# A hybrid encoder layer on one core: where a product is added in the first two column pairs, and at what pace the second batch's attention is issued

## The chip, the core and the metric

One NeuronCore of one Trainium2 chip. The core has a matrix engine (TensorE, PE in the profile), three engines for element-wise work (VectorE or DVE, ScalarE or ACT, GpSimd or POOL), a queue that issues transfers (SyncE or SP), and sixteen DMA engines. The metric is device time of one execution in microseconds (us), as the median of three runs.

## What is computed

Two batches, a "prompt" of 512 rows and a "sample" of 1024 rows, both 1024 wide, go through one layer with shared weights, in float32:

```python
h = rmsnorm(x); z = h @ w_in                # columns: q, k, v, conv a, conv b
a_out = window_attention(q, k, v)           # |q-k| <= 128, 8 heads, 2 kv heads, bias table, sink
c = silu(layernorm(dwconv31(ca * sigmoid(cb))))
x = x + concat(a_out, c) @ w_out
h = rmsnorm(x)
u = dwconv3(h @ w_up)                       # 2 * 2816 columns: gates, then values
x = x + (silu(u_gate) * u_value) @ w_down
y = rmsnorm(x)
```

## The kernel before

**Products.** A float32 product is made of three matmuls on a split of each operand into a rounded part and a remainder: hi·hi, hi·lo, lo·hi. A split is a cast on ScalarE (the hi part) and a subtraction on VectorE or GpSimd (the lo part). A matmul has 128x128 weights and 512 moving columns.

**Stages.** (1) Input projections of both batches, with the prompt's attention and convolution between them. (2) The prompt's output projection. (3) The prompt's up-projection, 22 steps `ffn_step(k)`, each with a gate and a value column block of 128. The sample's attention and the rest of its long convolution are issued between these matmuls. (4) The sample's output projection: for each block `i` of 128 rows two halves of 512 columns (`out_half`, lines 796 to 798), after `conv_norm` of that block. (5) The sample's up-projection, 22 column pairs `j`, by a Winograd form of Strassen's method: seven products per pair (`first` to `seventh`, lines 1221 to 1223) in place of eight. (6) The down-projection of both batches, and the last norm.

**What sets the order.** In stages 1 to 4 the program is written with a pace: `tick()` is called between groups of matmuls, adds `pace["rate"]` to a credit, and for each whole unit of credit draws one step from the deque `side`. A scheduler then orders the instructions of each engine by its own model of their times, so that the written order is only a wish there. In stage 3 `side` holds `sample()`: 100 steps of the sample's attention (`scores`, `values`), then the loads and splits of `w_out` (`load_cat`, `split_wo`), then `conv_norm` of the first two sample blocks (`fitted(4)`, `fitted(5)`). `tick()` is called 8 times per step `k`, and the rate is RD = 0.55. The deque `late` holds the rest of the sample's convolution; it is empty from k = 19. Of the attention's 100 steps 83 are written by then, and 96 by the end of stage 3. Stage 4 then draws what is missing before its first block: 17 steps, the last of the attention, the loads and eight splits among them.

**The attention's chain.** Per pair of a block and a kv head: scores on TensorE (line 650); bias and row minimum on VectorE (654); exponential on ScalarE (663); reciprocal on VectorE (665); scaling on ScalarE (669) and GpSimd (671); transposes on TensorE (692); a split by ScalarE (694) and VectorE (695); values on TensorE (706, 707); copies out (714 to 718). Attention has three PSUM banks, a0 to a2. A split of `w_out` is a cast at line 828 and a subtraction at line 829.

**`conv_norm`.** Transposes on TensorE (755), statistics on VectorE (760, 761), a root on GpSimd (146, 147), scaling on VectorE (764), transposes back (770), four small scalings on ScalarE (776) and a tanh (777), then lines 778 (VectorE), 779 (ScalarE, hi part) and 780 (VectorE, lo part). Lines 755 and 770 write the banks a0 to a2 too. Of the eight weight blocks of an output half, the last four are the result of `conv_norm`; the first four come from the attention.

**The first two pairs.** At the start of stage 5 pairs 0 and 1 are written out side by side, and four engines keep the written order, between which the scheduler may still put later work. A pair has two double banks: `x` (gates) and `wy`, whose left half W takes the fifth and then the third product, and whose right half Y takes the sixth and seventh. `fifth(j)` ends with a ScalarE copy of W into SBUF, `p5` (1322). `y_sum(j)` adds `p5` to Y, `third(j)` accumulates onto W and adds `u2` to it; both additions are the VectorE line 1071, on the same tile `wy`. `gate_part(j)` reads `x` with one ScalarE pass (1337) and two VectorE passes (1338, 1339); when the last has read it, the bank of `x` is free, and `first(j + 2)` takes it. `sums_up(j)` are five subtractions at line 1074 on raw weights.

```python
def y_sum(j):
    Y = st[j]["wy"][:, R]
    add(Y, Y, st[j].pop("p5")[:])

def third(j):
    s = st[j]
    W = s["wy"][:, L]
    prod(W, j, 3, False, True)
    add(W, W, s.pop("u2")[:])
```

Of the kernel before, what the change touches and what calls it, by code (L numbers as in the profile page):

```python
# [39 lines left out]
RA, RB, RBO, RD, RN, RE = 1.2, 0.8, 2.5, 0.55, 0.8, 0.9  # L40
# [23 lines left out]
LK = 1  # L64
# [44 lines left out]
def tile_hybrid_encoder(ctx: ExitStack, tc: tile.TileContext, xs, rel_bias, norm_attn_g, w_in,  # L109
# [173 lines left out]
    mid = []  # L283
    side, pace = deque(), dict(rate=0.0, due=0.0, conv=0.0, credit=0.0, late=0.0)
# [44 lines left out]
    convs, late, kept = deque(), deque(), {}  # L329
# [673 lines left out]
    def ffn_step(k):  # L1003
        want_up_raw(k + 1, 1)
        ug = up_half(k, 0)
        want_up(k + 1, 0)
        uv = up_half(k, 1)
        want_up_raw(k + 2, 0)
        want_up(k + 1, 1)
        gate(k, ug[0], uv[0])  # L1010
# [15 lines left out]
    def sample():  # L1026
        for _ in units_of_sample:
            yield 0.0
            if at[0] >= KL and not wor:
                for kc in range(0, KC, 2):  # L1030
                    load_wo_pair(kc, 0)
        kt.clear(), vt.clear(), qt.clear(), bias.clear()
        use.update(norm="a")
        pace.update(rate=RN)
        load_cat(4)
        for kc in range(KC):
            load_wo(kc, 1)
            split_wo(kc, 0, kc % 4 < DW2)
            yield 0.0
        drain(late)  # L1040
        yield from fitted(4)
        for kc in range(KC):
            if kc == 2:
                load_cat(5)
            split_wo(kc, 1, kc % 4 < DW2)
            yield 0.0
            if kc == WN:
                yield from fitted(5)

    pace.update(rate=RD, late=0)  # L1050
    for k in range(NJ):
        at[0] = k
        if k == LK:
            pace.update(late=CD)
        if k == 0:
            side.append(sample())
        ffn_step(k)
# [12 lines left out]
    def add(out, a, b, eng=None):  # L1070
        (eng or nc.vector).tensor_tensor(out, a, b, op=ALU.add)  # L1071

    def sub(out, a, b, eng=None):
        (eng or nc.vector).tensor_tensor(out, a, b, op=ALU.subtract)  # L1074
# [105 lines left out]
    def block_up(j, half, k):  # L1180
        return uraw[j, half][:, 4 * k:4 * k + 4, :].rearrange("p k c -> p (k c)")
# [10 lines left out]
    def split_up(j, *which, apart=False):  # L1192
        if j >= NJ:
            return
        for i in which:
            if i == 7:
                held = third_sum.pop(j)
                src = held[:]
            else:
                src = block_up(j, *{1: (0, 0), 2: (0, 1), 6: (0, 0), 4: (0, 1), 5: (1, 0), 3: (1, 1)}[i])  # L1200
            if not apart and any(s[0][0] in "qc" for s in sb.free):
                t = sb.tile([2, NT], F32R)
                hi, lo = Part(t, 0), Part(t, 1)
            else:
                hi, lo = sb.tile([NT], F32R), sb.tile([NT], F32R)
            ops[j, i] = hi, lo
            nc.scalar.copy(hi[:], src)  # L1207
            sub(lo[:], src, hi[:].bitcast(F32), nc.gpsimd)
            held = None
            done.add((j, i))  # L1210
        for half, pair in ((0, (6, 4)), (1, (5, 3))):
            if (j, half) in uraw and all((j, i) in done for i in pair):
                uraw.pop((j, half))

    def prod(out, j, i, start, stop, between=None):
        whi, wlo = ops.pop((j, i))
        go = dict(skip_group_check=not start)
        for c in range(4):
            hi, lo = A[i, c]
            s = slice(c * P, (c + 1) * P)  # L1220
            nc.tensor.matmul(out, whi[:, s], hi[:], start=(start and c == 0), stop=False, **go)  # L1221
            nc.tensor.matmul(out, whi[:, s], lo[:], start=False, stop=False, **go)  # L1222
            nc.tensor.matmul(out, wlo[:, s], hi[:], start=False, stop=(stop and c == 3), **go)  # L1223
            if j == NJ - 1:
                A.pop((i, c))
            if between is not None:
                next(between, None)
# [89 lines left out]
    def fifth(j):  # L1317
        if j < NJ:
            s = st[j]
            prod(s["wy"][:, L], j, 5, True, True)  # L1320
            s["p5"] = sb.tile([NT])
            nc.scalar.copy(s["p5"][:], s["wy"][:, L])
# [11 lines that stand above are left out]
    def dwconv(src, f):  # L1334
        w = lambda t: fw[:, t * 44 + f:t * 44 + f + 1]
        u = sb.tile([W2])
        nc.scalar.activation(u[:], src[:], AF.Identity, scale=w(1), bias=fb[:, f:f + 1])
        nc.vector.scalar_tensor_tensor(u[:, 1:W2], src[:, 0:W2 - 1], w(0), u[:, 1:W2], op0=ALU.mult, op1=ALU.add)  # L1338
        nc.vector.scalar_tensor_tensor(u[:, 0:W2 - 1], src[:, 1:W2], w(2), u[:, 0:W2 - 1], op0=ALU.mult, op1=ALU.add)  # L1339
        return u  # L1340

    def gate_part(j):
        s = st[j]
        ug = s["ug"] = dwconv(s.pop("x"), j)
        t = s["t"] = sb.tile([W2])
        nc.scalar.activation(t[:], ug[:], AF.Tanh, scale=0.5)
# [113 lines left out]
    seventh(1, None, False)  # L1460
    sums_up(2)
    fifth(0)
    y_sum(0)
    gate_part(0)
    fifth(1)
    y_sum(1)
    by_hand.__exit__(None, None, None)
    by_hand = tc.manual_schedule(engines={mybir.EngineType.PE})
    by_hand.__enter__()
    gate_part(1)  # L1470
    third(0)
    split_up(2, 5)
    value_part(0)
    first(2)
    split_up(2, 6, apart=True)
    third(1)
    split_up(2, 7)
    fifth(2)
    split_up(2, 4, 3)
# [399 lines left out]
```

## Time and profile before

| what | value |
|---|---|
| runs | 1488.01, 1488.84, 1489.47 us; median 1488.84 |
| profiled execution | 1487.68 us, of which the span from first to last instruction is 1485.9 us |
| TensorE busy | 1467.1 us, 99% of the span, 6688 matmuls |
| VectorE busy | 1115.6 us, 75% |
| ScalarE busy | 807.7 us, 54% |
| GpSimd busy | 793.9 us, 53% |
| moved by DMA | 228.17 MB, 153 GB/s over the span |

Rows of instructions read: start in us from the span's start, duration in us, engine, line, operation, out<-in by the program's names (for a matmul: out<-moving,weights), shape, count. A bracket at the end is the time for which the engine was idle before it and what it waited for. Matmuls overlap in the array, so that a matmul's duration (0.39 us with 512 columns) is longer than the distance to the next one. A view of stretches has a row for each: its length, then each engine's busy time and number of instructions, then the TensorE clock that was granted (1.00 is full speed), the share of the DMA engines and GB/s.

### The profile page before, as it was taken

The page shows a single profiled execution, that of the slowest core. Times are in us where ns is not written, and L with a number is a line of the kernel's source. Part 1 is how long each engine was busy: PE and PEld are TensorE (multiplying, and loading weights), DVE is VectorE, ACT ScalarE, POOL GpSimd, SP SyncE. Part 2 cuts the span into 40 slices and gives each one's busy share as a digit, 9 for nine tenths or more (in the row PEclk, how much of TensorE's full clock was granted, in tenths as well). Part 3 has the DMA queues.
Part 4 walks back from the last instruction along what each step waited for, and adds up shares of the span by engine and source line. Part 5 has one row for each costly group of instructions (what it writes and reads, how often), then busy time and mean ns, then how long its engine had stood idle before and what let it go on. Part 6 is the DMA issues. An engine that isn't in the chain of part 4 may idle for free. (4 is left out here: it accounts for less than half of the span.)

```text
span 1485.9 us, 19792 instructions
## 1 busy us (share of the span) xinstructions
PE 1467.1 (99%) x6688; PEld 1207.9 (81%) x6688; DVE 1115.6 (75%) x1500; ACT 807.7 (54%) x1432; POOL 793.9 (53%) x697
## 2 busy tenths in 40 slices
PE   9999999999999999999999999999999999999998
PEld 7788887878888888778877888888888888888886
DVE  6877845648988888675598888888887856578873
ACT  7534555467778776654565455454455553433355
POOL 3564453338779766322547666666654341135556
PEclk9999999999999999999999999999999999999999
DMA  9555331844444454663114433333332394356744
GB/s 368 193 152 143 106 106 30 245 159 140 122 143 135 130 181 140 205 219 111 71 57 144 141 130 127 127 124 123 129 127 92 147 335 157 123 190 220 226 159 162
DMA packets 124624, 228.17 MB, mean 154 GB/s; under 512 B 20419, under 2 KB 45763, under 8 KB 124396
## 3 DMA queue, kind: packets, MB, share of 16 engines
q1 hardware_dynamic: 124092, 226.37, 46.6%
q8 instruction: 52, 0.85, 0.2%
q10 hardware_dynamic: 432, 0.56, 0.1%
q14 instruction: 48, 0.39, 0.1%
HBM read 166.83 MB, written 61.10 MB: 153 GB/s over the span
## 5 line engine op out<-in xcount | busy, mean ns | idle before, releaser
L163 POOL TENSOR_TENSOR q<-q,q 128x1024 fp32r<-128x1024 f32 x66 | 158.9, 2408 | 67.9 <-ACT q L162 42.9
L1074 POOL TENSOR_TENSOR q<-q,q 128x512 fp32r<-128x512 f32 x82 | 124.5, 1526 | 125.6 <-ACT q L1207 116.2
L1074 DVE TENSOR_TENSOR h<-h,h 128x512 fp32r<-128x512 f32 (+1 forms) x161 | 135.3, 870 | 55.9 <-ACT h L1082 23.4
L1575 PE MATMUL w<-h,h 128*128 128x512 f32 x432 | 168.1, 389 | 0.0
L1577 PE MATMUL w<-h,h 128*128 128x512 f32 x432 | 168.1, 389 | 0.0
L1576 PE MATMUL w<-h,h 128*128 128x512 f32 x412 | 160.3, 389 | 0.0
L1074 POOL TENSOR_TENSOR h<-h,h 128x512 fp32r<-128x512 f32 (+1 forms) x46 | 67.5, 1468 | 144.9 <-ACT h L1558 121.8
L1221 PE MATMUL w<-h,q 128*128 128x512 f32 x350 | 138.1, 394 | 3.7 <-DVE w L1071 3.2
L1223 PE MATMUL w<-h,q 128*128 128x512 f32 x350 | 136.4, 390 | 0.0
L1222 PE MATMUL w<-h,q 128*128 128x512 f32 x350 | 136.3, 389 | 0.0
L1082 ACT CAST h<-h 128x512 fp32r<-128x512 f32 x116 | 69.3, 620 | 103.5 <-DVE h L1074 35.2
L315 PE MATMUL b<-h,q 128*128 128x512 f32 x312 | 123.0, 395 | 1.2 <-ACT h L461 0.6
L317 PE MATMUL b<-h,q 128*128 128x512 f32 x312 | 122.6, 393 | 0.0
L316 PE MATMUL b<-h,q 128*128 128x512 f32 x312 | 122.3, 392 | 0.0
L315 PE MATMUL u<-h,q 128*128 128x512 f32 x272 | 106.8, 393 | 0.0
L316 PE MATMUL u<-h,q 128*128 128x512 f32 x272 | 106.8, 393 | 0.0
L317 PE MATMUL u<-h,q 128*128 128x512 f32 x272 | 106.7, 392 | 0.0
L162 ACT CAST q<-q 128x1024 fp32r<-128x1024 f32 x66 | 69.1, 1048 | 53.1 <-PE u L316 16.7
L352 DVE SCALAR_TENSOR_TENSOR c<-d,cvw,c 128x512 f32<-128x512 f32 x128 | 95.9, 749 | 1.6
L344 POOL TENSOR_TENSOR h<-h,h 128x512 f32<-128x512 f32 x62 | 81.6, 1318 | 27.1 <-ACT h L343 22.6
L1575 PEld LDWEIGHTS w<-h,h 128*128 128x128 f32 x432 | 81.1, 188 | 17.0
L1577 PEld LDWEIGHTS w<-h,h 128*128 128x128 f32 x432 | 81.1, 188 | 16.6
(462 smaller groups left out, 3995.5 us busy)
## 6 DMA issues: line engine op xcount, KB each, us to landing
q<-in_laid_w_up SPq DMA_DIRECT2D x88, 512.0 KB, 3.7
ga<-q SPq DMA_DIRECT2D x65, 256.0 KB, 2.3
h<-gap SPq DMA_DIRECT2D x57, 256.0 KB, 3.7
h<-ga SPq DMA_DIRECT2D x57, 256.0 KB, 3.6
h<-in_w_down SPq DMA_DIRECT2D x52, 256.0 KB, 3.5
q<-in_laid_w_in SPq DMA_DIRECT2D x22, 512.0 KB, 3.9
gap<-h SPq DMA_DIRECT2D x44, 256.0 KB, 2.3
q<-in_x_sample SPq DMA_DIRECT2D x15, 512.0 KB, 6.8
```

The source lines that it names most:

```text
L163: (nc.vector if dve else nc.gpsimd).tensor_tensor(lo[:], raw[:], hi[:].bitcast(F32), op=ALU.subtract)
L315: nc.tensor.matmul(out, whi[:, kc, :], hi[:], start=(kc == 0), stop=False)
L316: nc.tensor.matmul(out, whi[:, kc, :], lo[:], start=False, stop=False)
L317: nc.tensor.matmul(out, wlo[:, kc, :], hi[:], start=False, stop=(kc == KC - 1))
L352: nc.vector.scalar_tensor_tensor(acc[:], src(t), w(t), acc[:], op0=ALU.mult, op1=ALU.add)
L1074: (eng or nc.vector).tensor_tensor(out, a, b, op=ALU.subtract)
L1221: nc.tensor.matmul(out, whi[:, s], hi[:], start=(start and c == 0), stop=False, **go)
L1222: nc.tensor.matmul(out, whi[:, s], lo[:], start=False, stop=False, **go)
L1223: nc.tensor.matmul(out, wlo[:, s], hi[:], start=False, stop=(stop and c == 3), **go)
L1575: nc.tensor.matmul(out, sh[:, c], th[:], start=(p == 0 and not seeded), stop=False, **go)
L1576: nc.tensor.matmul(out, sh[:, c], tl[:], start=False, stop=False, **go)
L1577: nc.tensor.matmul(out, sl[:, c], th[:], start=False, stop=(p == NPAIR - 1), **go)
```

## The change

Two edits. The first sets the pace of `side` to RE = 0.9 in stage 3, as soon as `late` is empty and no convolution is open. That holds from k = 19, so that 90 steps of the attention are written before k = 20 (88 before the change), 98 before k = 21 (92), and at the end of stage 3 all 100 and the first four splits of `w_out`; stage 4 draws 9 steps before its first block in place of 17. The second edit writes `y_sum(j)` behind `third(j)` for j = 0 and 1, and `third(0)` ahead of `gate_part(1)`. Lines after 1055 have numbers that are higher by 2 in the changed kernel.

```diff
--- before.py
+++ after.py
@@ -1052,6 +1052,8 @@
         at[0] = k
         if k == LK:
             pace.update(late=CD)
+        if k > LK and not late and not mid:
+            pace.update(rate=RE)
         if k == 0:
             side.append(sample())
         ffn_step(k)
@@ -1460,20 +1462,20 @@
     seventh(1, None, False)
     sums_up(2)
     fifth(0)
-    y_sum(0)
     gate_part(0)
     fifth(1)
-    y_sum(1)
     by_hand.__exit__(None, None, None)
     by_hand = tc.manual_schedule(engines={mybir.EngineType.PE})
     by_hand.__enter__()
+    third(0)
+    y_sum(0)
     gate_part(1)
-    third(0)
     split_up(2, 5)
     value_part(0)
     first(2)
     split_up(2, 6, apart=True)
     third(1)
+    y_sum(1)
     split_up(2, 7)
     fifth(2)
     split_up(2, 4, 3)
```

What the scheduler makes of it is seen in three places. In the names below the first number is the buffer's, the last a running number.

**VectorE, first two pairs.** `w0` and `w1` are the banks `x` of pairs 0 and 1, `w2` and `w3` their `wy`; `q2`, `q12` are raw weights of pair 2, `q6`, `q7` and `h50_1338`, `q3` of pairs 3 and 4. Before:

```order
L1074 TENSOR_TENSOR q2_6_7791<-q2_6_7791,q12_5_7789 128x512
L1074 TENSOR_TENSOR q12_5_7789<-q2_6_7791 128x512
L1074 TENSOR_TENSOR q12_5_7789<-q12_5_7789 128x512
L1071 TENSOR_TENSOR w2_3_7739<-w2_3_7739,h50_1307_7899 128x512
L1338 SCALAR_TENSOR_TENSOR q14_1308_7902<-w0_1_7559,fw_264,q14_1308_7902 128x1023
L1074 TENSOR_TENSOR h50_1338_8184<-q3_10_8012 128x512
L1338 SCALAR_TENSOR_TENSOR q13_1311_7926<-w1_2_7574,fw_264,q13_1311_7926 128x1023
L1339 SCALAR_TENSOR_TENSOR q14_1308_7902<-w0_1_7559,fw_264,q14_1308_7902 128x1023
L1074 TENSOR_TENSOR q3_10_8012<-q3_10_8012,q10_9_8010 128x512
L1071 TENSOR_TENSOR w2_3_7739<-w2_3_7739,d0_1291_7793 128x512
L1339 SCALAR_TENSOR_TENSOR q13_1311_7926<-w1_2_7574,fw_264,q13_1311_7926 128x1023
```

And now:

```order
L1076 TENSOR_TENSOR q2_6_7791<-q2_6_7791,q12_5_7789 128x512
L1076 TENSOR_TENSOR q6_7_7857<-q7_8_7859 128x512
L1076 TENSOR_TENSOR q12_5_7789<-q2_6_7791 128x512
L1076 TENSOR_TENSOR q12_5_7789<-q12_5_7789 128x512
L1340 SCALAR_TENSOR_TENSOR q10_1308_7901<-w0_1_7559,fw_264,q10_1308_7901 128x1023
L1340 SCALAR_TENSOR_TENSOR q8_1311_7938<-w1_2_7574,fw_264,q8_1311_7938 128x1023
L1341 SCALAR_TENSOR_TENSOR q10_1308_7901<-w0_1_7559,fw_264,q10_1308_7901 128x1023
L1073 TENSOR_TENSOR w2_3_7739<-w2_3_7739,d0_1291_7793 128x512
L1341 SCALAR_TENSOR_TENSOR q8_1311_7938<-w1_2_7574,fw_264,q8_1311_7938 128x1023
L1073 TENSOR_TENSOR w2_3_7739<-w2_3_7739,h5_1307_7899 128x512
```

The addition of `p5` (`h50_1307`, now `h5_1307`) to `w2` stood ahead of the passes over `w0`; it now stands behind the addition of `u2` (`d0`). One subtraction for pair 3 (`q6<-q7`) has moved ahead of the two on `q12`, two for pair 4 have moved back, and the passes over `w0` and `w1` follow each other. TensorE keeps its order: fifth(0), fifth(1), third(0), first(2), third(1), fifth(2), each of 12 matmuls; the first matmul of third(0) and that of third(1) waited for VectorE and now wait for ScalarE.

**ScalarE, end of stage 3.** `u0_339` (now `u0_342`) is the last gate or value block of the prompt. Line 694 splits the transposed probabilities of the last but one attention unit. Before:

```order
L981 ACTIVATE b0_340_6421<-h40_1039_6377 128x512
L828 CAST h24_1075_6507<-q6_934_5671 128x512
L663 ACTIVATE h58_1026_6281,s5_1024_6271<-h58_1026_6281,s2_1023_6270 128x257
L828 CAST h32_1072_6501<-q6_934_5671 128x512
L828 CAST h16_1069_6495<-q12_933_5669 128x512
L828 CAST h12_1066_6489<-q12_933_5669 128x512
L965 ACTIVATE h33_1042_6416<-u0_339_6381,vecs_83,fw_264 128x512
L663 ACTIVATE h53_1028_6305,s5_1024_6271<-h53_1028_6305,s2_1023_6270 128x257
L694 CAST h7_1035_6351<-a1_336_6346 128x512
L663 ACTIVATE h54_1027_6299,s5_1024_6271<-h54_1027_6299,s2_1023_6270 128x257
L828 CAST h36_1089_6557<-h2_1056_6469 128x512
L694 CAST h22_1037_6366<-a2_337_6361 128x512
```

And now:

```order
L663 ACTIVATE h5_1023_6242,s5_1021_6232<-h5_1023_6242,s2_1020_6231 128x257
L694 CAST h56_1028_6285<-a1_333_6280 128x512
L663 ACTIVATE h54_1025_6260,s5_1021_6232<-h54_1025_6260,s2_1020_6231 128x257
L828 CAST h47_1054_6441<-q0_931_5665 128x512
L828 CAST h30_1089_6557<-h0_1053_6439 128x512
L663 ACTIVATE h58_1024_6254,s5_1021_6232<-h58_1024_6254,s2_1020_6231 128x257
L965 ACTIVATE h36_1062_6475<-u0_342_6432,vecs_83,fw_264 128x512
L694 CAST h41_1030_6300<-a2_334_6295 128x512
L669 ACTIVATE h2_1022_6236<-h2_1022_6236,s5_1021_6232 128x256
L669 ACTIVATE h5_1023_6242<-h5_1023_6242,s5_1021_6232 128x256
L669 ACTIVATE h58_1024_6254<-h58_1024_6254,s5_1021_6232 128x256
L828 CAST h41_1057_6453<-q3_932_5667 128x512
```

Four casts of line 828 stood between the four exponentials of the last unit (663), and the first split (`h7_1035`) behind the third of these (`h53`); it now (`h56_1028`) stands ahead of the third, and two casts stand between. On VectorE three subtractions of line 829 stood ahead of the last two bias rows (654); now none stands among the four.

**TensorE and ScalarE, first blocks of stage 4.** `a0` to `a2` are the shared banks; `c0`, `b1`, `u1`, `u0` take output halves. `h44_1077` (now `h54_1077`) and `h14_1105` are hi parts from `conv_norm` of the first and second sample block. TensorE before, where the first block's transposes back (line 770, `a2_345`) stand, and, 22 products later, where their result is first used:

```order
L796 MATMUL u1_351_6691<-h60_1095_6581,h51_1051_6459 128x512
L796 MATMUL c0_346_6550<-h21_1063_6483,h51_1051_6459 128x512
L796 MATMUL b0_356_6813<-h21_1063_6483,h9_1118_6660 128x512
L770 MATMUL a2_345_6529<-ident_82,h23_1083_6527 128x128 x4
L755 MATMUL a0_347_6612<-ident_82,h26_1107_6610 128x128 x4
L797 MATMUL c0_346_6550<-h40_1064_6484,h51_1051_6459 128x512
L798 MATMUL c0_346_6550<-h21_1063_6483,h10_1052_6460 128x512
```

```order
L796 MATMUL u0_353_6748<-h60_1095_6581,h49_1091_6567 128x512
L755 MATMUL a2_350_6670<-ident_82,h8_1117_6658 128x128 x4
L770 MATMUL a1_348_6626<-ident_82,h30_1111_6624 128x128 x4
L796 MATMUL c0_346_6550<-h12_1066_6489,h44_1077_6511 128x512
L797 MATMUL c0_346_6550<-h34_1067_6490,h44_1077_6511 128x512
L797 MATMUL u1_351_6691<-h41_1096_6582,h51_1051_6459 128x512
L798 MATMUL u1_351_6691<-h60_1095_6581,h10_1052_6460 128x512
```

And now:

```order
L798 MATMUL u0_354_6762<-h9_1095_6581,h4_1092_6568 128x512
L770 MATMUL a2_345_6529<-ident_82,h2_1083_6527 128x128 x4
L770 MATMUL a1_348_6626<-ident_82,h45_1111_6624 128x128 x4
L755 MATMUL a2_350_6664<-ident_82,h50_1117_6652 128x128 x4
L755 MATMUL a1_353_6746<-ident_82,h0_1128_6727 128x128 x4
L796 MATMUL c0_346_6550<-h21_1066_6489,h54_1077_6511 128x512
L797 MATMUL c0_346_6550<-h42_1067_6490,h54_1077_6511 128x512
L796 MATMUL u1_352_6706<-h52_1097_6592,h54_1077_6511 128x512
L797 MATMUL u1_352_6706<-h18_1098_6593,h54_1077_6511 128x512
L770 MATMUL a0_351_6691<-ident_82,h5_1123_6676 128x128 x4
L796 MATMUL b1_349_6643<-h21_1066_6489,h14_1105_6608 128x512
L798 MATMUL c0_346_6550<-h21_1066_6489,h58_1078_6512 128x512
```

ScalarE before, and now:

```order
L828 CAST h55_1099_6596<-h38_1068_6493 128x512
L776 ACTIVATE h20_1084_6534<-a2_345_6529,vecs_83 128x2x64 x4
L777 ACTIVATE h43_1085_6535<-h20_1084_6534 128x512
L828 CAST h48_1097_6592<-h33_1065_6487 128x512
L779 CAST h44_1077_6511<-h43_1085_6535 128x512
L776 ACTIVATE h35_1112_6631<-a1_348_6626,vecs_83 128x2x64 x4
L777 ACTIVATE h1_1113_6632<-h35_1112_6631 128x512
L779 CAST h27_1105_6608<-h1_1113_6632 128x512
```

```order
L828 CAST h34_1101_6600<-h39_1071_6499 128x512
L776 ACTIVATE h17_1084_6534<-a2_345_6529,vecs_83 128x2x64 x4
L776 ACTIVATE h24_1112_6631<-a1_348_6626,vecs_83 128x2x64 x2
L828 CAST h16_1103_6604<-h53_1074_6505 128x512
L776 ACTIVATE h24_1112_6631<-a1_348_6626,vecs_83 128x2x64 x2
L777 ACTIVATE h27_1085_6535<-h17_1084_6534 128x512
L777 ACTIVATE h25_1113_6632<-h24_1112_6631 128x512
L779 CAST h54_1077_6511<-h27_1085_6535 128x512
L779 CAST h14_1105_6608<-h25_1113_6632 128x512
```

The transposes back of both blocks now follow each other, with no product between them and the first use of their result, and the small scalings of both blocks stand in a row ahead of either tanh. All products on the attention's part of five output halves (60 matmuls) stand ahead of them.

## Prediction

> **What bounds the kernel now.** I read the page's busy table first, then the waits of TensorE, then the granted clock over stretches, and last the single rows where a wait stands.
>
> ```profile
> span 1485.9 us, 19792 instructions
> PE 1467.1 (99%) x6688; PEld 1207.9 (81%) x6688; DVE 1115.6 (75%) x1500; ACT 807.7 (54%) x1432; POOL 793.9 (53%) x697
> ```
>
> TensorE is busy for 1467.1 of 1485.9 us, so what another engine saves counts only where TensorE waits for it. The waits of TensorE (engine, line waited at, releaser; total, times, longest) name two places at which the change works:
>
> ```profile
> PE w L1221 <- DVE w L1071: 3.2, 2, 2.4
> PE a L706 <- ACT h L694: 2.0, 1, 2.0
> ```
>
> The first is in the first two pairs, the second at the end of stage 3. The stretches around them, with one of stage 4 between, show what each wait draws behind it (the number after the last count in brackets is the granted clock):
>
> ```profile
> 625.00:635.00 10.00, 7.76 (x36) 5.34 (x34) 9.33 (x18) 7.32 (x17) 2.52 (x3) 0.83 0.96 331
> 631.00:634.40 3.40, 3.20 (x9) 1.83 (x8) 3.36 (x7) 2.71 (x7) 1.30 (x2) 0.50 1.01 389
> 645.00:655.00 10.00, 10.00 (x50) 8.35 (x49) 7.27 (x13) 5.05 (x11) 1.48 (x4) 1.00 0.25 82
> 770.00:780.00 10.00, 7.61 (x27) 5.50 (x26) 9.79 (x13) 4.07 (x6) 2.58 (x2) 0.83 0.00 0
> 774.40:777.80 3.40, 3.40 (x9) 2.42 (x8) 3.40 (x5) 0.14 (x1) 0.00 (x0) 0.50 0.00 0
> ```
>
> Behind each of the two waits lie 3.4 us at a clock of 0.50, in which 1.7 us of work is lost. Stage 4 at 645 to 655 has full clock and no gap.
>
> **Edit 1, the end of stage 3.** TensorE, ScalarE and VectorE there:
>
> ```profile
> 625.33 0.39 PE L317 MATMUL u<-h,q 128*128 128x512 f32 x1
> 625.55 0.40 PE L650 MATMUL a<-q,h 128*128 128x256 f32 x2
> 626.71 0.60 PE L692 MATMUL a<-ident,h 128*128 128x128 f32 x4
> 627.07 0.48 PE L650 MATMUL a<-q,h 128*128 128x256 f32 x2
> 629.60 0.50 PE L706 MATMUL a<-h,h 128*128 128x512 f32 x1 [2.04 <-ACT h L694]
> 642.98 0.60 PE L770 MATMUL a<-ident,h 128*128 128x128 f32 x4
> ...
> 624.60 1.65 ACT L828 CAST h<-q 128x512 fp32r<-128x512 f32 x3
> 626.28 0.78 ACT L965 ACTIVATE h<-u,vecs,fw 128x512 f32<-128x512 f32 x1
> 628.47 0.51 ACT L663 ACTIVATE h<-h,s 128x257 f32<-128x257 f32 x1 [1.42 <-DVE s L654]
> 628.98 0.56 ACT L694 CAST h<-a 128x512 fp32r<-128x512 f32 x1
> 632.68 1.30 ACT L669 ACTIVATE h<-h,s 128x256 f32<-128x256 f32 x3
> ...
> 625.55 2.43 DVE L829 TENSOR_TENSOR h<-q,h 128x512 fp32r<-128x512 f32 x3
> 627.90 0.47 DVE L654 CUSTOM_DVE_ANT_0 h<-a,h,nsink 128x256 f32<-128x256 f32 x1
> ```
>
> The chain reads backwards: L706 waited for the split L694 (628.98), which stands behind an exponential L663 (628.47), which waited for the bias row L654 (627.90), which stood behind three subtractions L829 that took 2.43 us. Matmuls of 512 columns start 0.22 to 0.23 us apart (625.33 to 625.55), four transposes take 0.36 (626.71 to 627.07). From 625.55 to 642.98 are 17.43 us; the order has 42 products there (42 x 0.225 = 9.45), 20 transposes (20 x 0.09 = 1.80) and 4 matmuls of L650 (0.45), in all 11.70. So 5.7 us are lost in this stretch, 1.7 of them to the clock.
>
> In the new order no L829 stands among the last L654, and the first split L694 is one exponential earlier. What is late next is ScalarE. From the end of the transposes (some 626.4) to the product that uses the first remaining w_out cast, it has to do L694 0.56, L663 0.51, two L828 (1.65 / 3 = 0.55 each), L663 0.51, L965 0.78, L694 0.56, three L669 1.30 and a L828 0.55: 5.87, so 632.3. TensorE's own work to there (10 products, 16 transposes, L650) is 3.9 from 625.8 on, so 629.7. It waits 2.6 in all, in pieces at L706, L692 and L796. Term: 2.6 - 5.7 = **-3.1**. Bounds: -5.7 if all waits go; -1.1 if VectorE is as late as before (the wait of 2.04 stays and joins the 2.6: 4.6 lost).
>
> Attention steps also issue on the other queues. GpSimd (scaling, L671) is busy 2.52 of 10 us in this stretch, so an earlier step finds it free: 0. SP's transfers are the tight queue: a DMA share of 0.96. Loads of the first sample block's convolution rows and of w_out move against each other there. The new order needs those rows only behind 60 products (13.5 us), so that hides their lateness. A late w_out load is not hidden; its price stands under the next part.
>
> **Edit 1, the first blocks of stage 4.** In before, the first use of the result of L770 stood 22 products behind it. Now only transposes stand between: 16 from the start of the first L770, 16 x 0.09 = 1.44 us. The chain that they must cover, shown on the second block of before:
>
> ```profile
> 649.52 0.60 PE L770 MATMUL a<-ident,h 128*128 128x128 f32 x4
> 650.16 1.51 ACT L776 ACTIVATE h<-a,vecs 128x128 f32<-128x128 f32 x4 [1.63 <-PE a L770]
> 651.70 0.63 ACT L777 ACTIVATE h<-h 128x512 f32<-128x512 f32 x1
> 653.09 0.62 ACT L779 CAST h<-h 128x512 fp32r<-128x512 f32 x1 [0.76 <-DVE h L778]
> ...
> 649.72 0.70 DVE L760 BATCH_NORM_STATS2 s<-a 128x6 f32<-128x512 f32 x1
> 651.58 0.81 DVE L764 TENSOR_SCALAR h<-a,s,s 128x512 f32<-128x512 f32 x1 [0.95 <-POOL s L147]
> 652.37 0.69 DVE L778 SCALAR_TENSOR_TENSOR h<-h,h 128x512 f32<-128x512 f32 x1
> ...
> 642.98:656.65 13.67, 13.67 (x70) 11.39 (x70) 9.28 (x16) 6.66 (x14) 1.83 (x5) 1.00 0.40 123
> ```
>
> One block alone takes 4.19 (649.52 to 653.09 + 0.62). In the new order of ScalarE the eight small scalings of both blocks and a w_out cast stand ahead of the first tanh: 0.64 (649.52 to 650.16) + 2 x 1.51 + 0.55 + 0.63 + 0.69 + 0.62 = 6.15. TensorE waits 6.15 - 1.44 = 4.7 in one piece. The second block's result follows by VectorE's L760, L764 and L778, 0.70 + 0.81 + 0.69 = 2.20, against 1.26 of products: 0.94 more. In before, the 13.67 us of the last row hold 50 products and 19 transposes of the order, 11.25 + 1.71 = 12.96: 0.7 lost. Term: 4.7 + 0.9 - 0.7 = **+4.9**. Bounds: +2.1 if only a block's own chain counts (4.19 - 1.44 - 0.7); +6.9 if the cast among the scalings waits for its load. Of such a load the trace shows the median from issue to landing:
>
> ```profile
> h<-in_laid_w_out SPq DMA_DIRECT2D x20, 256.0 KB, 4.5
> ```
>
> I add 2, somewhat under half of these 4.5 us. I take +4.9, since it is the sum of rows in the order that ScalarE keeps.
>
> **The clock.** Waits of 2.04 and 2.39 in one piece were each followed by 3.4 us at 0.50; one of 0.84 (781.41 below) was not. The handover's pieces should be short (0), the 4.7 is long: 1.7. But at half clock the 1.26 of products before the second block take 2.52, which swallows that block's 0.94. Term: 1.7 - 0.9 = **+0.8**; bounds 0 and +3.4 (both places).
>
> [...]
>
> **Edit 2, the first two pairs.** TensorE, VectorE and ScalarE:
>
> ```profile
> 770.34 0.39 PE L1223 MATMUL w<-h,q 128*128 128x512 f32 x1
> 773.12 0.50 PE L1221 MATMUL w<-h,q 128*128 128x512 f32 x1 [2.39 <-DVE w L1071]
> 777.38 0.66 PE L1221 MATMUL w<-h,q 128*128 128x512 f32 x1
> 781.41 0.50 PE L1221 MATMUL w<-h,q 128*128 128x512 f32 x1 [0.84 <-DVE w L1071]
> ...
> 770.97 1.49 DVE L1074 TENSOR_TENSOR q<-q 128x512 f32<-128x512 f32 x2
> 772.37 0.69 DVE L1071 TENSOR_TENSOR w<-w,h 128x512 f32<-128x512 f32 x1
> 772.97 1.27 DVE L1338 SCALAR_TENSOR_TENSOR q<-w,fw,q 128x1023 f32<-128x1023 f32 x1
> 775.96 1.27 DVE L1339 SCALAR_TENSOR_TENSOR q<-w,fw,q 128x1023 f32<-128x1023 f32 x1
> ...
> 768.04 0.59 ACT L1322 COPY h<-w 128x512 f32<-128x512 f32 x1 [1.78 <-PE w L1223]
> ```
>
> These rows are the last matmul of fifth(1), then the first of third(0), of first(2) and of third(1). The addition L1071 (772.37) held third(0). Now third(0) needs only ScalarE's copy, done at 768.63, so it starts at 770.56 and issues 12 matmuls to 773.27; the 2.39 and, at third(1), the 0.84 go. What is late next is first(2), which takes the bank w0 once the last pass over it has read it. In before that pass ended at 775.96 + 1.27 = 777.23, and the half clock covered it: first(2) came at 777.38. Now VectorE has three subtractions from 770.97 on (3 x 0.75 = 2.25, to 773.2), then three passes one behind another (w0, w1, w0: 1.2 + 1.2 + 1.27), to 776.9. So first(2) starts at 776.95, having waited 3.7 us, and third(1) at 776.95 + 12 x 0.225 = 779.65 in place of 781.41: -1.76. A wait longer than 2.39 should bring the half clock too, which takes 1.7 back. Term: **-0.1**. Bounds: -1.8 at full clock; +0.5 if the passes come one subtraction (0.75) later, less the 0.2 that the half clock's end leaves. The edit moves no transfer and nothing on GpSimd or SP; TensorE's order stays. Y gets its addition later, behind passes that TensorE does not wait for: 0.
>
> **Sum.** -3.1 + 4.9 + 0.8 - 0.1 = +2.5 us. The profiled execution took 1487.68 (span 1485.9, 1.8 around it), 1.16 below the median of 1488.84; 1490.2 against it is 1491.3 against the median. What a measurement can tell from no change is 0.2%, 3.0 us.
>
> **Rivals.**
> - *Slower by the chain of conv_norm.* The w_out cast between the small scalings waits 2 us for its load (+4.9 becomes +6.9), and the handover keeps its half clock (-3.1 + 1.7 = -1.4): -1.4 + 6.9 + 0.8 - 0.1 = +6.2, 1495.0. For it speaks the DMA share of 0.96; against it, that the share falls to 0.25 from 645 on. It decides once that cast starts more than 0.5 us late (2.5 + 0.5 = 3.0).
> - *Faster by the handover.* All of the 5.7 goes, and the chain behind L770 costs one block's 2.1, because small scalings of the second block find their input late and the first block's go ahead of them in time; clock full there: -5.7 + 2.1 + 0 - 0.1 = -3.7, 1485.1. For it: the 2.43 of L829 is gone from ScalarE's input. Against it: the engine keeps its order, and ScalarE's 5.87 at the handover stand in rows.
> - *The clock stays full.* Neither the wait of 4.7 nor that of 3.7 halves it: -3.1 + 4.9 + 0 - 1.8 = 0.0, 1488.8. For it: the half-clock stretches begin 1.4 and 1.3 us behind the wait's end, so the place of the wait in time may count; against it, both waits over 2 us had one. [...]
> That the change does nothing is excluded by the order, which moves at both places.
>
> **How the numbers follow.** Forecast (+0.8 to +4.5): 0.52, of which 0.30 lies within 0.2% and 0.22 above. Slower rival 0.21, faster rival 0.12 (0.11 beyond 0.2%), full clock 0.15. So faster 0.11, same 0.30 + 0.15 + 0.01 = 0.46, slower 0.22 + 0.21 = 0.43. The bounds of all terms add to -5.4 (-5.7 + 2.1 + 0 - 1.8) and +9.7 (-1.1 + 6.9 + 3.4 + 0.5). The range leaves out most of the faster rival and the upper part of the slower one: -2.4 to +6.6, 1486.4 to 1495.4. The forecast's own is 1489.6 to 1493.3.
>
> **What would show it.** In the profile after: no wait of L706 for L694 over 1.1 us; a new wait of 4 to 5 us of L796 or L797 for ScalarE (L779) near 647 to 655, with a second one behind; no wait at third(0) or third(1), and one of about 3.7 us at first(2) for VectorE's last pass over w0; a clock under 1.00 behind the last two. The prediction is wrong if TensorE finds the result of L779 ready, or if the handover still loses 5 us.

## The result: slower, and the profile after

| | before | after |
|---|---|---|
| median of 5 runs | 1488.84 us | 1495.57 us (1494.76 to 1500.02) |
| span of the profiled execution | 1485.9 us | 1493.8 us |

The ratio is 1.0057, 95% interval 1.0044 to 1.0069: 0.6% or 6.7 us slower. Forecast were 1491.3 us and a range up to 1495.4, so the time lies just above the range; by its size it is the forecast of the slower rival (+6.2), though not for that rival's reason.

The page after, and TensorE's waits (engine, line waited at, releaser; total, times, longest) around 626, 652 and 781 us:

```profile
span 1493.8 us, 19777 instructions
PE 1469.2 (98%) x6688; PEld 1209.8 (81%) x6688; DVE 1115.4 (75%) x1500; ACT 807.7 (54%) x1432; POOL 794.7 (53%) x697
```

```profile
PE b L796 <- DMA h<-catd: 2.0, 1, 2.0
...
PE a L755 <- ACT h L776: 2.4, 2, 1.3
PE c L796 <- ACT h L779: 1.2, 1, 1.2
...
PE w L1223 <- DVE q L1341: 4.0, 1, 4.0
```

The two waits of before are gone (L706 for L694, and the addition L1071). In their place stand three others: a transfer at the end of stage 3, ScalarE in the first blocks of stage 4, VectorE's pass over w0 in the first two pairs. The stretches around them (the third number from the end is the granted clock):

```profile
625.00:635.00 10.00, 7.87 (x40) 5.38 (x38) 7.45 (x16) 7.84 (x18) 2.28 (x4) 1.00 0.96 316
645.00:655.00 10.00, 6.18 (x33) 4.51 (x32) 7.21 (x15) 5.07 (x12) 3.42 (x6) 1.00 0.50 170
654.90:658.30 3.40, 3.40 (x11) 2.77 (x12) 2.94 (x6) 1.60 (x4) 1.52 (x2) 0.57 0.37 80
782.00:788.00 6.00, 4.62 (x11) 3.68 (x12) 6.00 (x8) 3.68 (x4) 0.00 (x0) 0.50 0.01 3
```

In before, 645 to 655 had TensorE busy for 10.00 of 10 us; now it is 6.18, with the half clock behind it (0.57 over 654.9 to 658.3, 0.50 over 655.4 to 658.8). The rows of TensorE there, and of ScalarE and VectorE:

```profile
648.75 1.09 PE L770 MATMUL a<-ident,h 128*128 128x128 f32 x8 [0.17 <-DVE h L764]
651.01 0.66 PE L755 MATMUL a<-ident,h 128*128 128x128 f32 x4 [1.16 <-ACT h L776]
652.93 0.66 PE L755 MATMUL a<-ident,h 128*128 128x128 f32 x4 [1.26 <-ACT h L776]
654.81 0.50 PE L796 MATMUL c<-h,h 128*128 128x512 f32 x1 [1.23 <-ACT h L779]
...
649.45 2.21 ACT L776 ACTIVATE h<-a,vecs 128x128 f32<-128x128 f32 x6 [5.02 <-PE a L770]
651.51 0.64 ACT L828 CAST h<-h 128x512 fp32r<-128x512 f32 x1
652.02 0.85 ACT L776 ACTIVATE h<-a,vecs 128x128 f32<-128x128 f32 x2
652.72 1.18 ACT L777 ACTIVATE h<-h 128x512 f32<-128x512 f32 x2
654.14 0.62 ACT L779 CAST h<-h 128x512 fp32r<-128x512 f32 x1 [0.24 <-DVE h L778]
```

From the start of L770 to the first use of its result are 6.06 us (648.75 to 654.81); 6.15 were forecast from before's rows. The 4.7 us of waiting forecast in one piece come in three (1.16, 1.26, 1.23), because the L755 between them need banks that the small scalings L776 still read: with the restarts, 4.2 us.

To compare kernels, lost time is summed at three places: the distance between the starts of two matmuls following one another, less the usual distance for the shape (0.227 us with 512 columns, 0.089 for a transpose), taken over equal amounts of TensorE's work. "Handover" is 9 us of work at the end of stage 3, the last 2 us of the prompt's up-projection and the 7 us behind it; "cover" is the next 18 us, which hold conv_norm of the first two sample blocks, "pairs" the 85 us around the first two pairs. The numbers come from each kernel's one profiled execution; the times from 5 to 12 runs beside 20 to 27 of before (after: 5 beside 5).

| kernel | against before, 95% | handover | cover | pairs |
|---|---|---|---|---|
| before | | 5.2 | 1.1 | 6.0 |
| after | 1.0044 to 1.0069 | 4.3 | 7.8 | 7.0 |
| e1 edit 1 alone | 1.0036 to 1.0063 | 7.1 | 9.0 | 6.2 |
| e2 edit 2 alone | 0.9992 to 1.0009 | 4.0 | 1.4 | 7.3 |
| e3 edit 2, w0 first | 0.9974 to 0.9992 | 4.6 | 1.1 | 5.2 |
| e4 edit 1, conv_norm before the splits | 1.0011 to 1.0029 | 10.0 | 0.6 | 6.1 |
| e5 edit 1, conv_norm behind four splits | 0.9987 to 1.0004 | 3.9 | 2.0 | 5.9 |
| e6 edit 1, earlier load | 1.0032 to 1.0057 | 3.6 | 9.8 | 6.6 |
| e7 before, conv_norm behind four splits | 1.0018 to 1.0041 | 5.5 | 5.4 | 6.2 |
| e8 edit 1 at rate 0.6 | 0.9975 to 0.9992 | 1.7 | 2.7 | 6.7 |
| e9 e3, subtractions on GpSimd | 0.9972 to 0.9991 | 5.2 | 1.3 | 4.5 |
| e10 e8 and e3 | 0.9952 to 0.9979 | 0.8 | 2.8 | 5.2 |
| e11 e8 and e9 | 0.9961 to 0.9983 | 0.8 | 3.4 | 4.5 |
| e12 after, conv_norm behind four splits | 0.9988 to 1.0006 | 3.6 | 1.9 | 7.8 |

Three cautions. Up to the last up-projection matmul these profiles had lost from 23.4 to 26.2 us, all but some 4 us of it in the first 350 us of work, where no edit acts; single spans therefore differ by up to 2.8 us for no reason of the change. The profile of e1 is that of the longest of its five executions (1497.10 us, their median is 1495.18), so its columns are likely too high. And the four kernels with before's order at the handover (before, e2, e3, e9) lose 4.0 to 5.2 there, so differences of 1 us in that column mean little.

For after the columns add up: start -0.4, handover -0.9, cover +6.7, the 110 us up to the pairs +0.5, pairs +1.0, behind them +1.0: +7.9, which is 1493.8 - 1485.9.

### The profile page after: what moved, and what is told of

Its sections match the earlier page's. It is cut to its first block, busy times and chain, and to the rows that moved or that the text cites. A ratio compares the mean times of both kernels' runs of the same rounds, so it can differ in the third digit from the quotient of the medians.

```text
span 1493.8 us, 19777 instructions
## 1 busy us (share of the span) xinstructions
PE 1469.2 (98%) x6688; PEld 1209.8 (81%) x6688; DVE 1115.4 (75%) x1500; ACT 807.7 (54%) x1432; POOL 794.7 (53%) x697
## 5 line engine op out<-in xcount | busy, mean ns | idle before, releaser
L1076 POOL TENSOR_TENSOR q<-q,q 128x512 fp32r<-128x512 f32 x80 | 119.5, 1502 | 129.9 <-ACT q L1209 121.8
L1223 PE MATMUL w<-h,q 128*128 128x512 f32 x342 | 135.6, 397 | 5.4 <-DVE q L1341 4.0
L1224 PE MATMUL w<-h,q 128*128 128x512 f32 x342 | 134.2, 392 | 0.0
L1225 PE MATMUL w<-h,q 128*128 128x512 f32 x342 | 134.2, 392 | 0.0
```

## Experiments

**Which edit carries it: e1 and e2.** e1 is edit 1 without edit 2:

```diff
+        if k > LK and not late and not mid:
+            pace.update(rate=RE)
```

> Edit 1 alone (the pace RE from k = 19; the first two pairs as in before). Theory A, that the two edits add up and that edit 1 is the cost: the handover loses as much as before (a load of the attention part in place of the cast), the chain of conv_norm behind L770 costs 4.3 us of waits and 1.7 of half clock: +6 us, between +5 and +7.5, and the waits at L755 for L776 and at L796 for L779 are there as in the changed kernel. Theory B, that most of the +6.7 us comes from the first two pairs or from an effect of the two edits on one another: +3 us or less.

1495.18 us against 1488.18, ratio 1.0050. All of the loss is there without edit 2; in the time theory A holds, and B falls. Theory A had the handover lose as much as before; its one profile shows 7.1 against 5.2, which the caution above makes uncertain. Its waits near 626 to 655:

```profile
PE b L796 <- DMA h<-catd: 3.1, 1, 3.1
PE a L755 <- ACT h L776: 2.4, 2, 1.3
PE c L796 <- ACT h L779: 1.2, 1, 1.2
```

The waits on ScalarE repeat those of after to 0.1 us. The one for the load was 2.0 us there and is 3.1 here.

e2 is edit 2 without edit 1: y_sum(j) behind third(j), as in the diff of the change.

> Edit 2 alone (y_sum behind third; the pace as in before). Theory A: third(0) and third(1) don't wait, first(2) waits 3.7 to 4.2 us for VectorE's last pass over w0 and a half clock follows: +0.8 us, between -0.2 and +1.5. Theory B (the pairs carry the loss): +3 us or more. Theory C (the half clock there depends on where in time the wait falls): -1.8 us with a clock of 1.00 behind the wait.

1487.95 us, ratio 1.0001: no difference that can be measured, though the pairs column is 1.3 higher than in before. The first matmul of first(2) in its profile:

```profile
776.14 0.77 PE L1221 MATMUL w<-h,q 128*128 128x512 f32 x1 [4.05 <-DVE q L1339]
```

The waits of 2.39 and 0.84 have turned into one of 4.05 at the place that the prediction named. Theories B and C fall.

**Is it the cover behind L770: e4, e5, e7, e12.** e5 is e1 with conv_norm of the first block drawn earlier:

```diff
         for kc in range(KC):
             load_wo(kc, 1)
             split_wo(kc, 0, kc % 4 < DW2)
             yield 0.0
-        drain(late)
-        yield from fitted(4)
+            if kc == 3:
+                drain(late)
+                yield from fitted(4)
```

> Edit 1, and conv_norm of the first sample block drawn behind four of the first eight w_out splits in place of behind all eight. The handover keeps its order (the first product takes the same loaded block), only the cover behind L770 grows from 1.4 to 6.0 us (7.1 for the second block). If the uncovered chain costs 7 to 9 us as the profiles of the changed kernel and of edit 1 alone show between the 607th and the 625th us of TensorE's work, 5 to 7 of them go: -5 to -7 against edit 1 alone, so between 0 and +2 against before. If the handover's wait for a load is the cost, +4 or more.

1487.46 us, ratio 0.9995: 0.3 us under before, where e1 was 7.0 above it. The waits for ScalarE are not in its list from 615 to 665 us any more; what is left there:

```profile
PE c L798 <- DMA h<-catd: 1.0, 1, 1.0
PE c L796 <- DMA h<-catd: 1.0, 1, 1.0
PE u L797 <- DVE h L829: 0.4, 1, 0.4
PE b L796 <- DMA h<-catd: 0.2, 1, 0.2
```

The cover column falls from 9.0 to 2.0. The handover falls too, from 7.1 to 3.9, so against e1 not all of the gain is cover; against after nearly all is (handover 4.3 and 3.9, cover 7.8 and 2.0). The first product waits only 0.2 us for its load here; the two waits of 1.0 behind it are for the other loads of attention parts, so the loads still cost nearly as much at the handover.

e7 does the opposite: the same edit on before, where it takes cover away (from 6.0 to 2.3 us), with the old pace.

> The kernel before with its own pace, and conv_norm of the first sample block drawn behind four splits. This makes the scheduler put the transposes back 2.3 us of products ahead of the first use (6.0 in before), with four small scalings of the second block between tanh and hi part on ScalarE: chain 0.64 + 1.51 + 0.63 + 1.51 + 0.62 = 4.9, so a wait of 2.6 us and perhaps a half clock: +2.5 to +4.5, without any change of pace. If cover behind L770 doesn't matter, within 1 us of before.

1492.32 us, ratio 1.0030: +4.6 us with no change of pace, just above what was expected; the cover column is 4.3 higher. The wait is there, at the two L755 that need the bank, with full clock behind it (products 0.23 us apart from 656.52 on):

```profile
PE a L755 <- ACT h L776: 2.3, 2, 1.6
```

With the restarts this is 2.6 us, the size that was expected. Some 2 us more of that column are lost between 638.6 and 643, around the last attention steps (L706, L707), whose splits stand among casts of w_out there. So uncovered transposes cost at either pace, though they are not the whole price of e7, and the same three lines of code make the kernel slower at one pace and repair it at the other, since what counts is where the scheduler then puts L770. Why the scheduler puts it there these runs do not show.

e12 is the changed kernel, both edits, with the edit of e5.

> The changed kernel, both edits at rate 0.9, with conv_norm of the first sample block drawn behind four splits in place of eight. If the cover behind L770 is the whole cause of the loss, this is as fast as before: between -1.5 and +1.5. If edit 2 adds a loss of its own, +1.5 to +3.

1487.62 us, ratio 0.9997. With cover behind L770 the whole loss of the changed kernel is gone, with edit 2 and rate 0.9 still in. The handover stays nearly as it was (3.6 for 4.3), though its waits for loads are other ones, the longest of 1.0 us; the cover column falls by 5.9.

e4 moved conv_norm further, ahead of all eight splits:

```diff
-        load_cat(4)
-        for kc in range(KC):
...
         drain(late)
+        load_cat(4)
         yield from fitted(4)
+        for kc in range(KC):
```

> Edit 1 with one thing more: the last part of the convolution and conv_norm of the first sample block are drawn ahead of the first eight splits of w_out, so that 8.6 us of products stand between L770 and the first use of its result (7.5 for the second block). If the uncovered chain behind L770 is the cost, -6 us against edit 1 alone, so between -1.5 and +1.5 against before, and no wait of L796 or L755 for ScalarE over 0.5 us near 650. If the handover carries the loss, +4 or more remains.

1491.29 us, ratio 1.0020: +3.1, between the two expectations. The cover column falls to 0.6, as expected, but the handover rises to 10.0, since w_out casts and attention splits now come behind conv_norm's work there:

```profile
PE a L706 <- ACT h L828: 2.0, 1, 2.0
PE a L706 <- ACT h L694: 1.2, 2, 0.8
PE a L707 <- DVE h L695: 1.0, 2, 0.8
```

The wait was moved, not removed; one between the two (e5) is better.

**Is it the load at the handover: e6, e8.** In after the first product of stage 4 waits for a load that SP issues late. SP's wait, and the rows of SP and TensorE (L722 stores the last attention result, L737 loads an attention part):

```profile
SPq L737 <- DVE s L654: 2.8, 1, 2.8
```

```profile
623.51 0.33 SPq L737 DMA_DIRECT2D h<-catd  x1
623.93 0.38 SPq L722 DMA_DIRECT2D catd<-h  x1
624.41 0.38 SPq L737 DMA_DIRECT2D h<-catd  x1
...
628.15 0.50 PE L796 MATMUL b<-h,h 128*128 128x512 f32 x1 [1.96 <-DMA h<-catd]
```

The load's buffer is given free at a bias row (L654), SP waits 2.8 us for that, the store goes ahead of the second half, and 3.7 us behind its issue (624.41) TensorE goes on (628.15). In before the first product took a part that had been loaded at 615.17. e6 is e1 with the first block's part loaded from k = 20 on, which makes that block the first product:

```diff
+            for i in (4,):
+                if at[0] >= 20 and (i, 0) not in cats:
+                    load_cat(i)
...
-        load_cat(4)
```

> Edit 1, and the load of the first sample block's attention part issued from k = 20 on in place of behind the last attention step; the first product of stage 4 then takes this block. If the handover of edit 1 waits for that load, the wait of 2.0 to 3.1 us at the first product goes and the handover loses about 3, as my prediction had it: -2 to -4 against edit 1 alone, +3 to +5 against before; the waits behind L770 stay as they are (cover 1.4 us). If the load is not the cause, +6 to +7.5 as edit 1 alone.

1494.84 us, ratio 1.0045: no gain that can be measured over e1, so the expectation of -2 to -4 was wrong. In the profile the wait for the load is gone and the handover loses 3.6, with these waits in its list from 615 to 665 us:

```profile
PE a L755 <- ACT h L776: 1.9, 2, 1.2
PE a L770 <- DVE h L764: 1.4, 1, 1.4
PE c L796 <- ACT h L779: 1.0, 1, 1.0
PE b L796 <- DVE h L983: 1.0, 1, 1.0
PE a L706 <- ACT h L694: 0.7, 1, 0.7
PE c L797 <- DVE h L829: 0.5, 1, 0.5
```

What the load had hidden comes out: pieces of 0.5 to 1.0 us for ScalarE and VectorE, and a later L764, which makes L770 1.4 us later (cover 9.8). Against after, whose load was 2.0 us late, the handover gains only 0.7. Against the profile of e1 it gains 3.5, but the medians of e1 and e6 are only 0.3 us apart, and e1's profile is likely too high, as said above. The load is the visible wait there, but taking that wait away does not make this kernel faster.

e8 is edit 1 with another number:

```diff
-            pace.update(rate=RE)
+            pace.update(rate=0.6)
```

> Edit 1 with a rate of 0.6 in place of 0.9. The order then has 5.5 us of cover behind the first L770 and 7.1 behind the second, as in before, and six w_out products ahead of the first L706. If edit 1 costs through cover and load alone, the waits behind L770 don't come: between -1.5 and +1.5 against before. If any higher pace costs by its traffic in stage 3, +2 or more.

1485.54 us, ratio 0.9984 (0.9975 to 0.9992): 2.2 us faster than before, a little beyond what was expected. In its list from 620 to 660 us stands:

```profile
PE a L770 <- DVE h L764: 0.5, 1, 0.5
PE c L796 <- ACT h L828: 0.2, 1, 0.2
```

The order has six w_out products just ahead of the first L706, and the handover loses 1.7 in place of 5.2, while the cover column is 1.6 higher than in before. The idea of edit 1 can thus win what the prediction had for it at the handover (-3.1; in this profile -3.5); at rate 0.9 the order is another one.

**The first two pairs: e3, e9.** e3 is edit 2 with VectorE's passes over w0 first:

```diff
-    sums_up(2)
     fifth(0)
     gate_part(0)
+    sums_up(2)
     fifth(1)
+    third(0)
+    y_sum(0)
     by_hand.__exit__(None, None, None)
...
-    third(0)
-    y_sum(0)
     gate_part(1)
```

> Edit 2 with gate_part(0) written ahead of sums_up(2), and held in order with third(0) and y_sum(0), so that VectorE makes both passes over w0 before the subtractions; the pace as in before. If the bank w0 is what first(2) waits for, the wait at first(2) goes (under 1 us), the half clock with it, and of the 5.8 us that before loses in the first two pairs some 5 come back: -4 to -5 us against before. If something else sets first(2), or the later subtractions make a new wait at fifth(2), between -1 and +1.

1485.84 us, ratio 0.9983 (0.9974 to 0.9992): -2.3, between the two expectations. The wait at first(2) and the half clock behind it are gone, but the pairs column falls only from 7.3 (e2) to 5.2, not to 1. The rest stands in small waits up to 860 us, while VectorE is full (third busy time of the second view, 765 to 780 and 780 to 800):

```profile
PE w L1221 <- ACT w L1292: 1.3, 3, 0.5
PE w L1221 <- ACT h L1301: 0.6, 1, 0.6
PE w L1221 <- ACT c L1337: 0.5, 1, 0.5
```

```profile
765.00:780.00 15.00, 14.52 (x64) 11.66 (x64) 14.75 (x15) 8.82 (x12) 7.47 (x6) 1.00 0.00 1
780.00:800.00 20.00, 19.55 (x85) 15.33 (x84) 19.13 (x20) 8.75 (x14) 10.12 (x7) 1.00 0.49 170
```

e9 takes sums_up(2) off VectorE:

```diff
-            sub(t[:], v1, v0)
...
+            e = nc.gpsimd if j == 2 else None
+            sub(t[:], v1, v0, e)
```

> As the kernel with edit 2 and the passes over w0 first (pace as in before), and the four subtractions of sums_up(2) on GpSimd in place of VectorE. Theory A: what came back there between 776 and 812 us (5 small waits) came back because VectorE is full (14.75 of 15 us) and the subtractions stand late; without them the waits shrink, 2 to 3.5 us more are won: -4 to -6 against before. Theory B, the splits behind the subtractions are late on GpSimd too (1.5 us each in place of 0.7): no gain over that kernel, -1 to -2.5.

1484.90 us, ratio 0.9982: no gain over e3 that can be measured, and 0.7 in the pairs column. With -3.3 against before it lies between the two theories' ranges. Theory A falls by its size. VectorE is still busy for 14.39 of 15 and 19.72 of 20 us there, as later work moves up, and GpSimd becomes full in the first stretch (the fifth busy time):

```profile
765.00:780.00 15.00, 13.84 (x60) 10.87 (x59) 14.39 (x15) 9.09 (x13) 14.84 (x10) 1.00 0.01 1
780.00:800.00 20.00, 20.00 (x90) 16.54 (x89) 19.72 (x18) 8.49 (x15) 10.30 (x8) 1.00 0.48 170
```

Whether the remaining 4.5 us are owed to VectorE as a whole or to the splits behind the subtractions is not settled.

**A version faster than both: e10, e11.** e10 has rate 0.6 and the order of e3, e11 that of e9.

> Rate 0.6 and edit 2 with the passes over w0 first, together. If the two places are independent their gains add: -2.2 and -2.3 give -4.5, between -3 and -6.

> The same with sums_up(2) on GpSimd. Theory A: -6 to -8 against before. Theory B: -3 to -5.

e10 is 1483.45 us against 1488.20, ratio 0.9966 (0.9952 to 0.9979); e11 1483.83, ratio 0.9972 (0.9961 to 0.9983). The gains of the two places add (-2.2 and -2.3 give -4.5; measured -4.8), and the subtractions on GpSimd bring nothing more (e11: -4.4), so theory A of e11 falls and its theory B holds.

## Why the prediction was wrong

- **The handover, -3.1: the step that failed.** In after it is -0.9, in e1's profile (likely too high) +1.9. Of the 4.2 us by which the time lies above the forecast, this term makes some 2.2 (-0.9 for -3.1); the columns put 1.0 more on the next term and 1.1 on the pairs, both near what they can resolve. The chain on ScalarE was worked out to 2.6 us of waiting, and e6, whose first product waits for no load, shows 2.2 us of waits for ScalarE and VectorE there, but with the restarts between the pieces 3.6 are lost, so even there the term would be -1.6. In after and e1 the first product's load is later still, and TensorE waits 1.96 and 3.12 us for it. The text looked at the loads of convolution rows and of w_out and found cover for the one; the load of the attention part, which the first product of the new order takes, it did not look at, and so put at nothing. What the runs show in place of one chain on ScalarE is several things late at once: with that load early (e6) pieces for ScalarE and VectorE remain, and the time stays as in e1.
- **The cover behind L770, +4.9 and +0.8 for the clock.** Right in mechanism, place and chain (6.06 us for 6.15). Measured +6.7 in all: the three waits and their restarts 4.2, half clock 1.7 (0.50 over 655.4 to 658.8) with the second block's 0.9 hidden in it as forecast, 0.6 for a late w_out subtraction at 643 (L829, 0.4 and its restart), which the sum did not have, and the rest in gaps under 0.35. e5 and e12 show that this term is the loss, e7 that it comes without the new pace too.
- **The pairs, -0.1.** Right within what can be timed (e2, 1.0001), and the wait of first(2) for w0 is there (4.04 for 3.7). Mis-sized: the three subtractions of 0.75 took 2.98 us in place of 2.25, and the half clock lasted for all of first(2) (0.50 over 781.7 to 788.5), as these rows show:

```profile
776.68 2.98 DVE L1076 TENSOR_TENSOR q<-q 128x512 f32<-128x512 f32 x3
781.97 1.27 DVE L1341 SCALAR_TENSOR_TENSOR q<-w,fw,q 128x1023 f32<-128x1023 f32 x1
...
783.38 0.77 PE L1223 MATMUL w<-h,q 128*128 128x512 f32 x1 [4.04 <-DVE q L1341]
787.36 0.63 PE L1223 MATMUL w<-h,q 128*128 128x512 f32 x1
```

- **The rivals.** The slower one had the right time with the wrong reason: the cast among the scalings (651.51) did not wait for its load, and the handover of after had full clock (1.00 over 627.5 to 631.0). The full clock and the faster one did not come.
- **The range.** It took its upper end from a rival at +6.2 with a cut at +6.6, while the bounds of the terms reached +9.7. With the handover's term at nothing, the other three give +5.6.

## What to carry to other kernels

When a change lets a scheduler reorder, count for each result the matrix work between its producer on TensorE and its first use, and compare it with the chain over the other engines; here 1.4 us of cover for a chain of 6.1 undid everything, and three lines that restored 6.0 us brought the time back. Do the same for the loads: ask which transfer the first instruction of a stage takes, when its buffer comes free and what is ahead of it in the issuing queue. And a gain at one wait is worth only what the next late thing leaves: e2, e3, e4 and e6 each removed the wait aimed at and found another behind it.

## What the clock did

A wait of 1.96 us (up to 628.15 in after) had full clock behind it (1.00), where before one of 2.04 was followed by 3.4 us at 0.50; behind one of 3.12 in e1 the clock was 0.50 too:

```profile
627.50:631.00 3.50, 2.78 (x12) 1.74 (x12) 1.55 (x4) 2.37 (x7) 0.00 (x0) 1.00 0.98 278
```

```profile
629.00:632.00 3.00, 2.76 (x9) 2.27 (x10) 0.59 (x1) 0.01 (x1) 0.00 (x0) 0.50 0.95 291
```

(The first row is of after, the second of e1.) In after, three waits of 1.16, 1.26 and 1.23 us with transposes between them had 0.50 behind them too, over 655.4 to 658.8, and the one of 4.04 us, which ended at 783.38, had 0.50 over 781.7 to 788.5, twice as long. So in these runs the length of one idle gap does not settle it; what does, they do not show.
